# Two modulation sums ordered behind the last turned block, and a Newton step issued on GpSimd, in a hybrid decoder layer

## The chip, the cores and the metric

The kernel runs on one core of one Trainium2 chip. A core has a matrix engine (TensorE, "PE" in the profile, with its weight loads shown as "PEld"), a vector engine (VectorE, "DVE"), a scalar engine (ScalarE, "ACT"), a general engine (GpSimd, "POOL"), and a queue engine (SyncE, "SP") that here only issues transfers between the memory of the chip and the core's own memory (SBUF). Matmul results go to eight PSUM banks of 128 x 512 float32 each.

The metric is the device time of one execution in microseconds (us). Three executions of the kernel before had a median of 737.48 us (737.26 to 738.08). The profiled execution is a fourth one.

## The reference

One post-norm decoder layer on 512 tokens of width 1024 in float32, conditioned on a vector c. What matters here are the modulation, the first LayerNorm, the up-projection behind it and the last LayerNorm:

```
mod = c @ w_ada + b_ada
sh1, sc1, gt1, sh2, sc2, gt2 = split(mod, 6)
u = x * (1 + sc1) + sh1
...                                  # two attention branches, gates, w_o
x = layer_norm(ALPHA * x + (1 + gt1) * attn_out, ln1_g, ln1_b)
u2 = x * (1 + sc2) + sh2
h = causal_depthwise_conv(u2 @ w_up, conv_w, conv_b)
h_gate, h_val = split(h, 2)
ffn_out = (silu(h_gate) * h_val) @ w_down
x = layer_norm(ALPHA * x + (1 + gt2) * ffn_out, ln2_g, ln2_b)

layer_norm(x) = (x - mean) * rsqrt(var + 1e-5) * g + b
```

## The kernel before, in words

**Matmuls.** Every float32 product is made of three passes of a narrower type: each operand is split into a high part (a copy to fp32r on ACT, `hi_of`) and the rest (a subtraction on DVE, `lo_of`, line 94). `mm3` (lines 140 to 142) multiplies high by high, high weight by low activation (`u2l`), and low weight (`wl`) by high activation.

**Weights.** `weights` (line 151) walks a list of items. A load of an item is issued on SP into one of five buffers `raw`, and waits there until the buffer's last reader has run. ACT then makes `wh` (line 203) and DVE makes `wl` (line 94). Among the items are slices of the modulation matrix: their "processing" is not a split but a sum over the row, `mod_sum` (line 226), a VectorE instruction over 128 x 1024 elements with an accumulator that is read out by a second, short one. Sums with a number `n` below 24 are held back and released behind the last `lo_of`; the eight with `n` from 24 on feed the gate `gt2`, which is wanted only in the down-projection, and had no such order.

**Order.** The transfers of SP keep the order of the program. On the other engines a scheduler puts the instructions in order when the kernel is built, by their dependencies and its own costs; `tc.issue_after(x)` adds an edge so that the instructions inside the block stand behind `x` on the engine of `x`. Each engine then runs its list strictly in order.

**Around the first LayerNorm.** The 512 tokens are four blocks of 128. `o_mm` (line 892) multiplies by w_o, `o_norm` (line 906) adds the residual (line 911), takes statistics (line 912) and calls `ln_stats` for mean and reciprocal root, and scales the rows (line 915). `o_turn` (line 918) transposes a block on PE (line 925), applies scale and shift on ACT (line 928, half 0) and DVE (line 929, half 1) and splits it into `u2h` and `u2l`, the moving operands of the up-projection. The first three up-projections (`NSPLIT`) are run in two halves of the tokens: `up_mm` over tokens 0 to 255 for all three, with the turning of block 3 in between, and then over tokens 256 to 511, which need blocks 2 and 3.

**`ln_stats`** (line 862) takes the mean and variance from the statistics (line 864), a square root on ACT (line 866), adds the epsilon (line 867), inverts (line 868), and makes one Newton step of two instructions over 128 x 1 (lines 869 and 870), all but the root on DVE. It is called for the four blocks of the first LayerNorm, for the first two blocks of the last one (`first_rows`), and for its last two (`tail`, line 1196).

**The end.** The last two blocks of rows are finished by `tail(2)` and `tail(3)`: a centering by line 1202, the multiplication with the reciprocal root by line 1206, and a transfer out on SP. The statistics of block 3 wait for the last matmuls of the program, which come in two pieces of 256 columns (lines 1305 and 1306).

Of the kernel before, what the change touches and what calls it, by code (L numbers as in the profile page):

```python
# [12 lines left out]
ALU = mybir.AluOpType  # L13
# [5 lines left out]
D = 1024  # L19
# [8 lines left out]
EPS = 1e-5  # L28
# [23 lines left out]
def layer_kernel(ctx: ExitStack, tc: tile.TileContext, out, xT, x, c8, wa0, wa1, bcol, w1, wct, wv, bf,  # L52
# [3 lines left out]
    V, S, G, PE = nc.vector, nc.scalar, nc.gpsimd, nc.tensor  # L56
# [14 lines left out]
    cnt, state = [0], {"load": 0, "proc": 0}  # L71

    def nm(s):
        cnt[0] += 1
        return f"{s}_{cnt[0]}"

    def bank():
        return pp.tile([P, 512], F32, name=nm("ps"), tag="ps")
# [8 lines left out]
    def fl(ap):  # L87
        return ap.bitcast(F32)

    def hi_of(o, i, scale=1.0):  # L90
        S.activation(o, i, AF.Copy, scale=scale)

    def lo_of(o, i, hi):
        state["read"] = V.tensor_tensor(o, i, fl(hi), ALU.subtract)  # L94
        return state["read"]
# [40 lines left out]
    def z(dt, s, shape=(P, 512)):  # L136
        return zp.tile(list(shape), dt, name=nm(s), tag="z", bufs=NZ)
# [86 lines left out]
    def mod_sum(w, col, wt, c, e, by=None):  # L224
        o = modr[:, w, col, e : e + 1]
        state["read"] = V.scalar_tensor_tensor(wt[:, c], wt[:, c], 1.0, cbc[:, c] if by is None else by, ALU.mult, ALU.mult, accum_out=o)  # L226
        return state["read"]
# [366 lines left out]

    def ada_proc(n):
        def f(r):
            mod_sum((4, 2, 3, 5)[n // 8], n % 8, r, slice(0, D), 0)
        f.late = n < 24
        return f

# [246 lines left out]
    u2h = u2p.tile([P, KT, 512], F32R, name="u2h", tag="u2h")  # L847
    u2l = u2p.tile([P, KT, 512], F32R, name="u2l", tag="u2l")
# [10 lines left out]
    G.memset(epsc, EPS)  # L859


    def ln_stats(st):
        mv = cons.tile([P, 8], F32, name=nm("mv"), tag="mv", bufs=2)
        V.bn_aggr(mv[:, 0:2], st)
        v, s, y, t = mv[:, 2:3], mv[:, 3:4], mv[:, 4:5], mv[:, 5:6]
        S.activation(s, mv[:, 1:2], AF.Sqrt, bias=epsc)
        V.tensor_scalar_add(v, mv[:, 1:2], EPS)
        V.reciprocal(y, s)
        V.scalar_tensor_tensor(t, y, y, v, ALU.mult, ALU.mult)
        V.scalar_tensor_tensor(y, t, -3.0, y, ALU.add, ALU.mult)  # L870
        return mv[:, 0:1], y

    def ln_row(n):
# [32 lines left out]
    def o_norm(i):  # L906
        xn, ps2 = o_st.pop(i)
        st = cons.tile([P, 2, 6], F32, name=nm("st"), tag="st", bufs=2)
        for e in range(2):
            ps = ps2[e]  # L910
            V.scalar_tensor_tensor(xn[e], xn[e], ALPHA, ps, ALU.mult, ALU.add)
            V.bn_stats(st[:, e, :], xn[e])
        mu, rs = ln_stats(st)
        for e in range(2):
            V.tensor_scalar(xn[e], xn[e], mu, rs, ALU.subtract, ALU.mult)
        x1.append(xn)

    def o_turn(i):
        tb = slice(i * P, (i + 1) * P)
        xn = x1[i]  # L920
        pts = [bank(), bank()]
        ufs = [z(F32, "uf2"), z(F32, "uf2")]
        for e in range(2):
            for q in range(4):
                PE.transpose(pts[e][:, q * P : (q + 1) * P], xn[e][:, q * P : (q + 1) * P], ident)
        for q in range(4):
            c = slice(q * P, (q + 1) * P)
            S.activation(ufs[0][:, c], pts[0][:, c], AF.Identity, bias=bm[:, q : q + 1], scale=gm[:, q : q + 1])
            V.tensor_scalar(ufs[1][:, c], pts[1][:, c], gm[:, q + 4 : q + 5], bm[:, q + 4 : q + 5], ALU.mult, ALU.add)
        for e in range(2):  # L930
            uf = ufs[e].rearrange("p (a b) -> p a b", b=P)
            hi_of(u2h[:, 4 * e : 4 * e + 4, tb], uf)
            lo_of(u2l[:, 4 * e : 4 * e + 4, tb], uf, u2h[:, 4 * e : 4 * e + 4, tb])

    def o_x1(i, e):
        if not lnr:
# [58 lines left out]
    for n in range(2 * FT):  # L995
# [7 lines left out]
        if n in (23, 27):  # L1003
            t = t13[(23, 27).index(n)][:, 0:512]
# [48 lines left out]
    for i in range(2, NB):  # L1053
        o_mm(i, range(KT))
        o_norm(i)
        for t in ((0, 1), (2,))[i - 2]:
            o_turn(t)
# [70 lines left out]
    for n in range(2 * FT):  # L1128
# [27 lines left out]
        t = z(F32, "cv")  # L1156
# [6 lines left out]
        if n % 2 == 1:  # L1163
            g, v = hc
# [18 lines left out]
    r = x1  # L1183
# [11 lines left out]

    def tail(i, st, pieces, eng):
        tb = slice(i * P, (i + 1) * P)
        mu, rs = ln_stats(st[:, 0 : len(pieces), :])
        for e, c0, c1 in pieces:
            c = slice(e * 512 + c0, e * 512 + c1)  # L1200
            v = r[i][e][:, c0:c1]
            V.scalar_tensor_tensor(v, v, mu, lnr[0][:, c], ALU.subtract, ALU.mult)
        for e, c0, c1 in pieces:
            c = slice(e * 512 + c0, e * 512 + c1)
            v = r[i][e][:, c0:c1]
            V.scalar_tensor_tensor(v, v, rs, lnr[1][:, c], ALU.mult, ALU.add)
            eng.dma_start(out[tb, c], v)
# [80 lines left out]
    for n, k in enumerate(wi):  # L1288
        w = weights(k)
        for a, p in enumerate(range(2 * n, min(FP - LATE, 2 * n + 2))):  # L1290
            t = ops[p][3]
# [5 lines left out]
    for i in range(2):  # L1297
        pieces = [(1, 0, 512)] if i == 0 else [(1, 0, 256), (1, 256, 512)]
        for n, (e, c0, c1) in enumerate(pieces):
            ps = bank()[:, 0 : c1 - c0] if i else W1[0]  # L1300
            for q in range(LATE):
                t = ops[FP - LATE + q][3]
                product(ps, t[:, top[i]], t[:, bot[i]], wc[q][0][:, c0:c1], wc[q][1][:, c0:c1], i == 1 and q == 0, q == LATE - 1, i == 0)
            v = r[2 + i][e][:, c0:c1]
# [70 lines left out]
```

## Time and profile before

| | |
|---|---|
| median of three executions | 737.48 us |
| profiled execution | 737.86 us |
| its span, first to last instruction | 736.1 us |
| PE busy | 725.6 us (99%) |
| DVE busy | 599.2 us (81%) |
| ACT busy | 390.0 us (53%) |
| POOL busy | 84.7 us (12%) |
| mean clock granted to PE | 0.998 of full speed |

The span is what the trace sees; the profiled execution's own time is 1.76 us longer. A row of the timeline gives the start in us from the span's beginning, the duration, engine, line, operation, the tile written and the tiles read with their shapes, and in brackets how long the engine stood idle before it and what released it. Instructions of one line that follow each other are merged into one row with a count.

### The profile page before, as it was taken

How to read it: one execution, taken by the hardware profiler on the slowest of the kernel's cores; microseconds unless marked ns; L12 is line 12 of the kernel's file. 1: busy time of each engine (PE TensorE's matmuls, PEld its weight loads, DVE VectorE, ACT ScalarE, POOL GpSimd, SP SyncE). 2: the span in 40 equal slices, each digit the busy share in tenths (PEclk: the TensorE clock that was granted, in tenths of full speed). 3: DMA queues.
4: the chain of work that ended last, by engine and by line, in shares of the span. 5: the costliest groups of instructions: out<-in, count | busy, mean ns of one | idle time of the engine just before them, and what ended most of it. 6: DMA issues, size and time to landing. Idle time of an engine off the chain costs nothing.

```text
span 736.1 us, 9841 instructions
## 1 busy us (share of the span) xinstructions
PE 725.6 (99%) x3441; PEld 606.6 (82%) x3441; DVE 599.2 (81%) x1048; ACT 390.0 (53%) x681; POOL 84.7 (12%) x139
## 2 busy tenths in 40 slices
PE   8999999999999999999999999999999999999995
PEld 5888888888888888888889888888888888888885
DVE  6878789778799896883597989977887778679996
ACT  4566476586886755432065554444454544346550
POOL 1026224343010000000000001000011001000010
PEclk9999999999999999999999999999999999999999
DMA  9943634522431232542074678577799767646733
GB/s 341 404 173 118 225 115 150 194 65 103 150 116 61 112 135 94 201 149 86 1 254 132 225 228 253 171 229 226 208 349 247 214 221 217 215 161 225 233 81 87
DMA packets 45346, 131.96 MB, mean 179 GB/s; under 512 B 6152, under 2 KB 6672, under 8 KB 45296
## 3 DMA queue, kind: packets, MB, share of 16 engines
q1 hardware_dynamic: 38032, 112.61, 44.3%
q0 software_dynamic: 4224, 10.30, 7.1%
q10 hardware_dynamic: 3040, 8.42, 3.1%
q8 instruction: 27, 0.44, 0.3%
q14 instruction: 23, 0.19, 0.1%
HBM read 118.39 MB, written 12.85 MB: 178 GB/s over the span
## 4 chain that ended last, share of the span: by engine, by line
PE 94%; DVE 3%; DMA 1%; ACT 1%; issue 0%; DVEq 0%; ACTq 0%
PE ps L140 19%; PE ps L141 19%; PE ps L142 19%; PE ps L342 5%; PE ps L1105 5%; PE ps L1107 5%; PE ps L1106 5%; PE ps L580 3%; PE ps L562 2%; PE ps L488 2%; PE ps L490 2%; PE ps L489 2%; PE ps L903 1%; PE ps L902 1%; PE ps L904 1%; PE ps L514 1%
## 5 line engine op out<-in xcount | busy, mean ns | idle before, releaser
L94 DVE TENSOR_TENSOR wl<-raw,wh 128x1024 fp32r<-128x1024 f32 (+2 forms) x114 | 136.6, 1200 | 34.7 <-ACT wh L203 33.5
L203 ACT ACTIVATE wh<-raw 128x1024 fp32r<-128x1024 f32 (+1 forms) x105 | 109.1, 1041 | 103.7 <-PE ps L141 37.6
L141 PE MATMUL ps<-u2l,wh 128*128 128x512 f32 (+1 forms) x376 | 141.2, 376 | 0.3 <-DVE u2l L94 0.3
L142 PE MATMUL ps<-u2h,wl 128*128 128x512 f32 (+1 forms) x376 | 141.1, 375 | 0.0
L140 PE MATMUL ps<-u2h,wh 128*128 128x512 f32 (+1 forms) x376 | 141.0, 376 | 0.0
L141 PEld LDWEIGHTS ps<-u2l,wh 128*128 128x128 f32 x376 | 70.8, 188 | 13.2 <-DVE u2l L94 0.5
L142 PEld LDWEIGHTS ps<-u2h,wl 128*128 128x128 f32 x376 | 70.8, 188 | 12.9
L140 PEld LDWEIGHTS ps<-u2h,wh 128*128 128x128 f32 x376 | 70.6, 188 | 12.7
L140 PE MATMUL ps<-uh,wh 128*128 128x512 f32 x200 | 79.5, 397 | 0.0
L142 PE MATMUL ps<-uh,wl 128*128 128x512 f32 x200 | 78.2, 391 | 0.0
L141 PE MATMUL ps<-ul,wh 128*128 128x512 f32 x200 | 77.9, 390 | 0.0
L1158 ACT ACTIVATE cv<-ps,cw 128x512 f32<-128x512 f32 x44 | 34.0, 773 | 49.1 <-PE ps L142 39.3
L1159 DVE SCALAR_TENSOR_TENSOR cv<-ps,cw,cv 128x511 f32<-128x511 f32 x44 | 32.8, 745 | 24.8 <-ACT cv L1158 24.7
L142 PEld LDWEIGHTS ps<-uh,wl 128*128 128x128 f32 x200 | 37.5, 188 | 8.5 <-DVE wl L94 0.2
L141 PEld LDWEIGHTS ps<-ul,wh 128*128 128x128 f32 x200 | 37.6, 188 | 7.4
L140 PEld LDWEIGHTS ps<-uh,wh 128*128 128x128 f32 x200 | 37.5, 188 | 7.3
L226 DVE SCALAR_TENSOR_TENSOR raw<-raw,cbc 128x1024 f32<-128x1024 f32 x32 | 39.6, 1238 | 0.0
L542 POOL TENSOR_TENSOR pt<-pt,om 128x127 f32<-128x127 f32 (+3 forms) x32 | 39.0, 1230 | 1.1 <-DVE om L541 1.0
L169 POOL DMA_DIRECT2D raw<-in_wdp x10 | 8.9, 890 | 246.4 <-DMA raw<-in_wdp 228.8
L1160 DVE SCALAR_TENSOR_TENSOR cv<-ps,cw,cv 128x510 f32<-128x510 f32 x44 | 32.7, 744 | 0.4
L1166 ACT ACTIVATE cv<-cv 128x512 f32<-128x512 f32 x22 | 13.9, 631 | 31.7 <-DVE cv L1160 31.7
L541 DVE TENSOR_TENSOR_SCAN om<-om,dg 128x127 f32<-128x127 f32 (+3 forms) x32 | 27.3, 913 | 3.6 <-ACT om L536 3.6
(234 smaller groups left out, 1555.3 us busy)
## 6 DMA issues: line engine op xcount, KB each, us to landing
raw<-in_wup SPq DMA_DIRECT2D x44, 512.0 KB, 4.5
raw<-in_wa SPq DMA_DIRECT2D x32, 512.0 KB, 3.6
raw<-in_wct SPq DMA_DIRECT2D x25, 512.0 KB, 4.4
raw<-in_wdp SPq DMA_DIRECT2D x20, 512.0 KB, 5.3
wa<-in_wa SPq DMA_DIRECT2D x15, 512.0 KB, 7.6
raw<-in_wdp SPq DMA_DIRECT2D x22, 256.0 KB, 4.3
raw<-t SPq DMA_DIRECT2D x22, 256.0 KB, 4.3
raw<-in_wdp POOLq DMA_DIRECT2D x10, 512.0 KB, 7.4
```

What stands on the lines that cost most here:

```text
L94: state["read"] = V.tensor_tensor(o, i, fl(hi), ALU.subtract)
L140: PE.matmul(ps, wh, ah, start=first, stop=False)
L141: PE.matmul(ps, wh, al, start=False, stop=False)
L142: return PE.matmul(ps, wl, ah, start=False, stop=last)
L203: state["hi"] = S.activation(h[:, 0:cols], r[:, 0:cols], AF.Copy)
L226: state["read"] = V.scalar_tensor_tensor(wt[:, c], wt[:, c], 1.0, cbc[:, c] if by is None else by, ALU.mult, ALU.mult, accum_out=o)
L342: PE.matmul(grp[g], w, u, start=j == 0 and n == 0, stop=j == KT - 1 and n == (1 if g == 7 else 2))
L542: G.tensor_tensor(pt[b][:, s : e - 1], pt[b][:, s : e - 1], om[:, s + 1 : e], ALU.mult)
L1105: PE.matmul(ps, ah, bh, start=first, stop=False, skip_group_check=onto)
L1106: PE.matmul(ps, ah, bl, start=False, stop=False, skip_group_check=onto)
L1107: return PE.matmul(ps, al, bh, start=False, stop=last, skip_group_check=onto)
L1158: S.activation(t, ps, AF.Identity, bias=cw[:, n, 3:4], scale=cw[:, n, 2:3])
```

## The change

Three edits. The modulation sums are put behind the last `lo_of` of `o_turn` (numbers from 24 on) or behind the last `lo_of` at all (below 24, which `release` did already). The two instructions of the Newton step become `tensor_scalar` with two per-partition scalars instead of `scalar_tensor_tensor`. And `ln_stats` takes an engine for the epsilon and the Newton step, which is GpSimd in `tail` and VectorE elsewhere.

```diff
     def ada_proc(n):
         def f(r):
-            mod_sum((4, 2, 3, 5)[n // 8], n % 8, r, slice(0, D), 0)
+            with tc.issue_after(state["turn" if n >= 24 else "read"].ins):
+                mod_sum((4, 2, 3, 5)[n // 8], n % 8, r, slice(0, D), 0)
         f.late = n < 24
         return f
...
-    def ln_stats(st):
+    def ln_stats(st, eng=V):
         mv = cons.tile([P, 8], F32, name=nm("mv"), tag="mv", bufs=2)
         V.bn_aggr(mv[:, 0:2], st)
         v, s, y, t = mv[:, 2:3], mv[:, 3:4], mv[:, 4:5], mv[:, 5:6]
         S.activation(s, mv[:, 1:2], AF.Sqrt, bias=epsc)
-        V.tensor_scalar_add(v, mv[:, 1:2], EPS)
+        eng.tensor_scalar_add(v, mv[:, 1:2], EPS)
         V.reciprocal(y, s)
-        V.scalar_tensor_tensor(t, y, y, v, ALU.mult, ALU.mult)
-        V.scalar_tensor_tensor(y, t, -3.0, y, ALU.add, ALU.mult)
+        eng.tensor_scalar(t, y, y, v, ALU.mult, ALU.mult)
+        eng.tensor_scalar(y, t, -3.0, y, ALU.add, ALU.mult)
         return mv[:, 0:1], y
...
-            lo_of(u2l[:, 4 * e : 4 * e + 4, tb], uf, u2h[:, 4 * e : 4 * e + 4, tb])
+            state["turn"] = lo_of(u2l[:, 4 * e : 4 * e + 4, tb], uf, u2h[:, 4 * e : 4 * e + 4, tb])
...
     def tail(i, st, pieces, eng):
         tb = slice(i * P, (i + 1) * P)
-        mu, rs = ln_stats(st[:, 0 : len(pieces), :])
+        mu, rs = ln_stats(st[:, 0 : len(pieces), :], G)
```

With the new edges the scheduler orders DVE and ACT anew around the turning of blocks 2 and 3. The first place is VectorE at the first three up-projection weights. `wl_3778`, `wl_3785` and `wl_3815` are the low parts for up-projections 0, 1 and 2; `xn_3676` is half 1 of block 3. Before:

```order
L94 TENSOR_TENSOR wl_3778<-raw_3767,wh_3777 128x1024
L94 TENSOR_TENSOR wl_3785<-raw_3769,wh_3784 128x1024
L911 SCALAR_TENSOR_TENSOR xn_3676<-xn_3676,ps_3680 128x512
L94 TENSOR_TENSOR wl_3815<-raw_3771,wh_3814 128x1024
L912 BN_STATS st_3729<-xn_3676 128x6
L929 TENSOR_SCALAR uf_722_3746<-ps_3744,gm,bm 128x128
```

On VectorE at the same place, now:

```order
L94 TENSOR_TENSOR wl_3778<-raw_3767,wh_3777 128x1024
L912 SCALAR_TENSOR_TENSOR xn_3676<-xn_3676,ps_3680 128x512
L94 TENSOR_TENSOR wl_3785<-raw_3769,wh_3784 128x1024
L913 BN_STATS st_3729<-xn_3676 128x6
L930 TENSOR_SCALAR uf_722_3746<-ps_3744,gm,bm 128x128
```

The residual of block 3 has moved ahead of `wl_3785`, and `wl_3815` has left this stretch. The second place is VectorE a little later, where block 2 (`uf_721`, `uf_722`) is split, block 3 is scaled (`xn_3675`, `xn_3676`) and turned (`uf_740`, `uf_741`), and the two sums over `raw_3775` and `raw_3979` stand. Before:

```order
L94 TENSOR_TENSOR u2l<-uf_721_3745,u2h 128x4x128
L915 TENSOR_SCALAR xn_3675<-xn_3675,mv_3734 128x512
L915 TENSOR_SCALAR xn_3676<-xn_3676,mv_3734 128x512
L94 TENSOR_TENSOR u2l<-uf_722_3746,u2h 128x4x128
L226 SCALAR_TENSOR_TENSOR raw_3775,modr<-raw_3775,cbc 128x1024
L226 SCALAR_TENSOR_TENSOR raw_3979,modr<-raw_3979,cbc 128x1024
L929 TENSOR_SCALAR uf_741_3845<-ps_3843,gm,bm 128x128 x4
L94 TENSOR_TENSOR u2l<-uf_740_3844,u2h 128x4x128
L94 TENSOR_TENSOR u2l<-uf_741_3845,u2h 128x4x128
L94 TENSOR_TENSOR wl_3982<-raw_3773,wh_3981 128x1024
```

On VectorE there, now:

```order
L94 TENSOR_TENSOR u2l<-uf_721_3745,u2h 128x4x128
L871 TENSOR_SCALAR mv_3734<-mv_3734 128x1
L94 TENSOR_TENSOR u2l<-uf_722_3746,u2h 128x4x128
L916 TENSOR_SCALAR xn_3675<-xn_3675,mv_3734 128x512
L916 TENSOR_SCALAR xn_3676<-xn_3676,mv_3734 128x512
L94 TENSOR_TENSOR wl_3815<-raw_3771,wh_3814 128x1024
L930 TENSOR_SCALAR uf_741_3845<-ps_3843,gm,bm 128x128 x4
L94 TENSOR_TENSOR u2l<-uf_740_3844,u2h 128x4x128
L94 TENSOR_TENSOR u2l<-uf_741_3845,u2h 128x4x128
L226 SCALAR_TENSOR_TENSOR raw_3775,modr<-raw_3775,cbc 128x1024
L226 SCALAR_TENSOR_TENSOR raw_3979,modr<-raw_3979,cbc 128x1024
L94 TENSOR_TENSOR wl_3982<-raw_3773,wh_3981 128x1024
```

The two sums have gone from ahead of the turning of block 3 to behind it, the second split of block 2 has gone ahead of the scaling of block 3, and `wl_3815` now stands between that scaling and the turning. On ScalarE, `wh_3814` went from ahead of the four `uf_721` instructions to behind them. On PE the first matmuls of up-projections 1 and 2 over tokens 256 to 511, which stood ahead of up-projection 0's second matmul there, went back to their own groups. The third place is VectorE at the last rows (block 3, `xn_3675` and `xn_3676`, with statistics `mv_6895`). Before:

```order
L864 BN_AGGR mv_6895<-st_6776 128x2
L867 TENSOR_SCALAR mv_6895<-mv_6895 128x1
L1202 SCALAR_TENSOR_TENSOR xn_3675<-xn_3675,mv_6895,ln_0_5201 128x512
L868 RECIPROCAL mv_6895<-mv_6895 128x1
L1202 SCALAR_TENSOR_TENSOR xn_3676<-xn_3676,mv_6895,ln_0_5201 128x256
L869 SCALAR_TENSOR_TENSOR mv_6895<-mv_6895 128x1
L1202 SCALAR_TENSOR_TENSOR xn_3676<-xn_3676,mv_6895,ln_0_5201 128x256
L870 SCALAR_TENSOR_TENSOR mv_6895<-mv_6895 128x1
L1206 SCALAR_TENSOR_TENSOR xn_3675<-xn_3675,mv_6895,ln_1_5203 128x512
L1206 SCALAR_TENSOR_TENSOR xn_3676<-xn_3676,mv_6895,ln_1_5203 128x256 x2
```

On VectorE there, now:

```order
L865 BN_AGGR mv_6895<-st_6776 128x2
L1203 SCALAR_TENSOR_TENSOR xn_3675<-xn_3675,mv_6895,ln_0_5201 128x512
L869 RECIPROCAL mv_6895<-mv_6895 128x1
L1203 SCALAR_TENSOR_TENSOR xn_3676<-xn_3676,mv_6895,ln_0_5201 128x256 x2
L1207 SCALAR_TENSOR_TENSOR xn_3675<-xn_3675,mv_6895,ln_1_5203 128x512
L1207 SCALAR_TENSOR_TENSOR xn_3676<-xn_3676,mv_6895,ln_1_5203 128x256 x2
```

And the end of GpSimd's list, now, where before nothing stood behind the transfers:

```order
L1266 DMA out<-xn_3459 128x512
L1266 DMA out<-xn_3460 128x512
L868 TENSOR_SCALAR mv_6828<-mv_6828 128x1
L870 TENSOR_SCALAR mv_6828<-mv_6828 128x1
L871 TENSOR_SCALAR mv_6828<-mv_6828 128x1
L868 TENSOR_SCALAR mv_6895<-mv_6895 128x1
L870 TENSOR_SCALAR mv_6895<-mv_6895 128x1
L871 TENSOR_SCALAR mv_6895<-mv_6895 128x1
```

Three instructions of each of the last two blocks (`mv_6828` is block 2) have left VectorE for GpSimd.

## Rows read from the trace of the kernel before

**Rows 1.** Waits of PE, whole run: engine line, releaser: us in total, times, longest

```profile
PE ps L141 <- DVE u2l L94: 0.3, 1, 0.3
```

**Rows 2.** DVE timeline, 381 to 392: start us, us, engine line op out<-in xcount

```profile
381.03 0.68 DVE L911 SCALAR_TENSOR_TENSOR xn<-xn,ps 128x512 f32<-128x512 f32 x1
381.63 1.22 DVE L94 TENSOR_TENSOR wl<-raw,wh 128x1024 fp32r<-128x1024 f32 x1
...
385.74 1.00 DVE L915 TENSOR_SCALAR xn<-xn,mv 128x512 f32<-128x512 f32 x2
386.66 0.69 DVE L94 TENSOR_TENSOR u2l<-uf,u2h 128x512 fp32r<-128x512 f32 x1
387.26 1.22 DVE L226 SCALAR_TENSOR_TENSOR raw<-raw,cbc 128x1024 f32<-128x1024 f32 x1
...
389.55 1.36 DVE L929 TENSOR_SCALAR uf<-ps,gm,bm 128x128 f32<-128x128 f32 x4
390.83 1.47 DVE L94 TENSOR_TENSOR u2l<-uf,u2h 128x512 fp32r<-128x512 f32 x2
```

**Rows 3.** PE timeline, 380 to 392

```profile
380.12 0.39 PE L904 MATMUL ps<-woh,ml 128*128 128x512 f32 x1
...
388.10 0.28 PE L142 MATMUL ps<-u2h,wl 128*128 128x256 f32 x1
...
390.73 0.52 PE L140 MATMUL ps<-u2h,wh 128*128 128x256 f32 x3
391.57 0.39 PE L141 MATMUL ps<-u2l,wh 128*128 128x256 f32 x1 [0.32 <-DVE u2l L94]
```

**Rows 4.** ACT timeline, the high part of the third up-projection weight

```profile
380.07 1.06 ACT L203 ACTIVATE wh<-raw 128x1024 fp32r<-128x1024 f32 x1 [0.21 <-DMA raw<-in_wup]
```

**Rows 5.** SP and DVE timelines: second sum's load, and an addition at 404

```profile
382.87 0.33 SPq L162 DMA_DIRECT2D raw<-in_wa  x1
...
404.44 0.69 DVE L956 TENSOR_TENSOR raw<-raw,raw 128x512 f32<-128x512 f32 x1
```

**Rows 6.** DVE and ACT timelines, last rows, 728 to the end

```profile
728.37 0.42 DVE L1305 TENSOR_TENSOR xn<-xn,ps 128x256 f32<-128x256 f32 x1 [0.29 <-PE ps L1107]
729.29 0.24 DVE L864 BATCH_NORM_AGGREGATE mv<-st 128x2 f32<-128x18 f32 x1
729.56 0.15 DVE L867 TENSOR_SCALAR mv<-mv 128x1 f32<-128x1 f32 x1
729.62 0.29 ACT L866 ACTIVATE mv<-mv,epsc 128x1 f32<-128x1 f32 x1 [4.95 <-DVE mv L864]
729.63 0.74 DVE L1202 SCALAR_TENSOR_TENSOR xn<-xn,mv,ln 128x512 f32<-128x512 f32 x1
730.29 0.16 DVE L868 RECIPROCAL mv<-mv 128x1 f32<-128x1 f32 x1
730.75 0.21 DVE L869 SCALAR_TENSOR_TENSOR mv<-mv 128x1 f32<-128x1 f32 x1
730.88 0.48 DVE L1202 SCALAR_TENSOR_TENSOR xn<-xn,mv,ln 128x256 f32<-128x256 f32 x1
731.27 0.15 DVE L870 SCALAR_TENSOR_TENSOR mv<-mv 128x1 f32<-128x1 f32 x1
731.46 1.54 DVE L1206 SCALAR_TENSOR_TENSOR xn<-xn,mv,ln 128x512 f32<-128x512 f32 x3
```

**Rows 7.** POOL timeline, three multiplications of the attention stage

```profile
56.75 2.66 POOL L542 TENSOR_TENSOR pt<-pt,om 128x127 f32<-128x127 f32 x1
...
60.24 0.63 POOL L542 TENSOR_TENSOR pt<-pt,om 128x255 f32<-128x255 f32 x1
...
60.87 1.08 POOL L542 TENSOR_TENSOR pt<-pt,om 128x511 f32<-128x511 f32 x1
```

**Rows 8.** POOL and DVE timelines, 67 to 71

```profile
67.77 2.06 POOL L542 TENSOR_TENSOR pt<-pt,om 128x511 f32<-128x511 f32 x1
...
68.82 2.10 DVE L94 TENSOR_TENSOR wl<-raw,wh 128x1024 fp32r<-128x1024 f32 x1
```

## Prediction

> **What bounds the kernel now.** I read the waits first, since the page has PE busy for 99% of the span. In the whole run PE waits once for data behind the start-up: 0.3 us, for a low part of block 3 (`u2l`) from DVE [rows 1]. So nothing that makes another engine quicker between the first microseconds and the last matmul can give more than that wait and what follows from it; and anything that makes a weight or an activation late costs in full. The timeline of PE shows the place: three matmuls that need only `u2h`, then a gap of 0.32 us, then a matmul that takes 0.39 where the same shape takes 0.28 [rows 3]. Wait and slow restart are 0.32 + 0.11 = 0.43 us. The timeline of DVE shows what the wait hangs on: two sums from 387.26 to 389.55, 2.29 us, then four scalings and the splits [rows 2]. Of these 2.29 us PE feels 0.43, because it had other matmuls to do.
>
> The second place is the end. Behind the last matmul DVE alone sets the time: subtraction and statistics of the last 256 columns from 728.37, aggregate, root, centering, Newton step, and from 731.46 the last multiplications, each followed by its transfer [rows 6]. There every microsecond of DVE is one of the time.
>
> **Part 1, the sums.** They leave the stretch ahead of block 3, but the order shows that they don't leave alone, so I follow DVE through it. The residual `xn_3676` now stands ahead of `wl_3785`. PE's last matmul for it ends at 380.12 + 0.39 = 380.51 [rows 3], so it starts near 380.5 instead of 381.03, with DVE idle for a moment before. One weight split stands between it and its statistics before and after, so all that follows is 0.5 us early. Then the second split of block 2 goes ahead of the two scalings of block 3: + 0.60 (from 386.66 to 387.26) [rows 2]. The scalings, done at 386.66 before, are done at 386.66 - 0.5 + 0.6 = 386.8, or up to 0.5 later, since ACT now makes the third `wh`, 1.06 us [rows 4], between block 2's scalings and its `u2h` and root, on which DVE waits. Only now comes `wl_3815`, 1.22 us [rows 2]: ready between 388.0 and 388.5. PE wanted it at 388.10 [rows 3]. So a new wait of 0 to 0.5 us comes in; I take 0.3 and the restart of 0.11 with it.
>
> Behind it the four scalings of block 3 take 1.28 (389.55 to 390.83), and with ACT's part the splits come at about 390.3 and 391.0. PE gets to block 3 at 390.73 plus the new wait, and wants the second split 1.5 us after the first (12 matmuls of 0.12, since 22 lie between 388.10 and 390.73). The old wait is gone. Sum of part 1: -0.43 + 0.41, about 0. Bounds: -0.43 if `wl_3815` is in time, and +0.3 if it is as late as 388.5 and its weight load adds some 0.2.
>
> The sums run from about 391. The second needs a load whose buffer is freed by `wl_3815`; it was issued at 382.87 and had landed when its sum began, half of 2.29 us behind 387.26, so 5.5 us later at most, and is now issued near 388.3 and lands by 393.8 [rows 2, 5]. Behind that sum on DVE stands `wl_3982`, which is ready some 2.5 us later, at 396 to 397; PE wants it after 72 more matmuls, near 399.6. On SP the next two transfers wait for the sums and start 4 to 5 us later; what they bring is added on DVE at 404.44 [rows 5]. If that came late, DVE would stand still for at most that long, and PE works on weights that were split before. I cost both at nothing; without this cover the price is the lateness, some 1 us.
>
> **Part 2, the form of the Newton step.** Two `scalar_tensor_tensor` of 0.21 and 0.15 become `tensor_scalar`, of which the nearest row is 0.15 [rows 6]. That is 0 to 0.06 us for each of six calls. They lie under PE's matmuls: nothing.
>
> **Part 3, the last rows on GpSimd.** DVE loses three instructions. What they hold up, from their start to the next one's: 0.07 (729.56 to 729.63), 0.13 (730.75 to 730.88), 0.19 (731.27 to 731.46) [rows 6]: 0.39 us. DVE is free for the last multiplications at 731.07 instead of 731.46. But these now wait for GpSimd, whose two last instructions wait for the reciprocal. The reciprocal ends at 730.29 - 0.07 + 0.16 = 730.38. So the chain DVE to GpSimd, two instructions, and back has 0.69 us for the full gain and 1.08 us before it costs.
>
> The trace of before has no such instruction on GpSimd. Two two-input ones with DVE not in the way take 0.63 at 255 and 1.08 at 511 elements [rows 7]: a line through them gives 0.2 at one element. A hand-over between engines is 0.09 (the aggregate's end, 729.29 + 0.24, to ACT's root, 729.62) [rows 6]. Two instructions and three hand-overs: 0.7 us, so the last multiplications start at 731.07: -0.39.
>
> Against that stands one thing that the trace shows. At 67.77 a GpSimd multiplication of 511 elements takes 2.06 instead of 1.08, and a DVE split under way beside it, with both inputs in SBUF, takes 2.10 instead of 1.22 [rows 2, 7, 8]: they hold each other up, and neither passes the other in the middle. The centerings by line 1202 also have two inputs in SBUF. If each GpSimd instruction must find a gap between them: the epsilon behind the 512-wide centering, done at 730.4; the first centering of 256 columns to 730.8; the next GpSimd instruction 731.0; the second centering 731.4; the last GpSimd instruction 731.6; multiplication at 731.65, +0.2. If DVE's three centerings all go first, three instructions and three hand-overs come after 731.07: 0.9 us, 731.97, +0.5. Between -0.39 and +0.5 I take +0.1, as the row at 68.82 is nearest.
>
> The Trainium skill has this as a rule ("SBUF — State Buffer", section "Who interferes with whom"): a VectorE instruction with two SBUF inputs and a GpSimd instruction that reads SBUF take a shared port in turn, whole instructions at a time. The trace agrees, with 2.10 us against 1.22; by the rule in full the last rows come out at the +0.2 above, without it at -0.39.
>
> Block 2's rows have the same chain. There DVE stands idle for 0.29 before 728.37 [rows 6] and loses 0.39 us of work, so 0.68 us of lateness cost nothing; the chain, with 512-wide centerings, is about that late. I cost it at 0, with +0.3 as the other end.
>
> **Sum.** 0 + 0 + 0.1, about 0.1 us on a profiled execution of 737.86 us. The three executions had a median of 737.48, 0.38 lower, so the forecast for a median is 737.5 us: no change that can be measured. A change below about 0.2%, 1.5 us, can't be told from none here.
>
> **The rivals.**
> - Both gains come in full: `wl_3815` in time and GpSimd within 0.69 us. -0.43 - 0.39 = -0.8: 736.7 us. For it: 0.2 us for a small GpSimd instruction; against it: rows 8, and the place of `wl_3815`. This is the most that the change can give, and still below 1.5 us. Chance 0.2.
> - Slower: GpSimd's chain becomes the bound of the last rows. Place: the last multiplications' wait. It costs from 1.08 us behind the reciprocal on. The first multiplication of GpSimd in the program, 127 elements, took 2.66 us beside DVE scans [rows 7]; one such instruction in the chain puts it at 0.09 x 3 + 0.2 + 2.66 = 3.1 us, +2.1: 739.6 us. Against it: the same line gives 0.2. Chance 0.07.
> - The late transfers stop DVE, and PE after it: +1: 738.5 us. Against it: DVE has a fifth of its time free. Chance 0.05.
> - The change does not do what it says: the pin concerns eight sums, of which two move; the other six stand where they stood. That is in the forecast.
>
> The Trainium skill ("GPSIMD Engine Reference", section "Instruction dispatch") adds about 6 us for the first call of a freshly loaded GpSimd routine; with that the time would be near 743. The trace does not bear it out for the plain instructions, whose first multiplication took 2.66 us.
>
> **How the numbers follow.** Forecast 0.68 (737.5, its own range 736.9 to 738.1), full gain 0.2, GpSimd 0.07, transfers 0.05. The range 736.6 to 738.6 takes in the full gain, both ends of the port's cost and the transfers, and leaves out GpSimd's long chain and small unknowns. Only the GpSimd case and part of the transfers are slower by over 0.2%: 0.08. No case here gives a gain of 1.5 us; for what I don't see I leave 0.04. Within: 0.88.
>
> **What would show it.** Right: PE's wait for `u2l` is gone and one for `wl`, 0.2 to 0.5 us, stands near 388; the sums lie at 391 to 395 and nobody waits for them; the last multiplications start 3.0 to 3.6 us behind the last matmul's subtraction (3.09 before). Wrong: PE shows no wait there and the last multiplications start 2.7 us behind (full gain); or DVE idles over 0.5 us for GpSimd in the last rows; or a new wait of PE stands between 391 and 728. A median below 736 or above 739 would mean that some other stage has changed.

## The result and the profile after

The changed kernel has a median of 738.99 us (738.63 to 740.45, 22 runs), the kernel before, timed beside it, 737.88 us (737.22 to 738.70, 22 runs): 1.11 us more, ratio 1.0016 with a 95% interval of 1.0010 to 1.0022. That is less than the 0.2% that I called measurable, but it lies above the predicted range, and with so many runs it is a loss and no noise. The profiled execution took 739.42 us, its span 737.6 us.

**The middle.** The waits of PE in the whole run, as engine, line and releaser, then us in total, times, longest:

```profile
PE ps L215 <- DVE warm L106: 1.2, 1, 1.2
PE ps L220 <- DVE chl L120: 1.0, 1, 1.0
PE ps L1106 <- DVE cv L1161: 0.3, 1, 0.3
PE ps L342 <- ACT uh L303: 0.3, 1, 0.3
```

The wait for `u2l` [rows 1] is gone. Three of these four lie in the first 15 us; the one at L1106, in the down-projection, is new. The timeline of DVE after, at the stretch of [rows 2] (start us, us, engine, line, operation):

```profile
386.36 1.00 DVE L916 TENSOR_SCALAR xn<-xn,mv 128x512 f32<-128x512 f32 x2
387.27 1.22 DVE L94 TENSOR_TENSOR wl<-raw,wh 128x1024 fp32r<-128x1024 f32 x1
388.41 1.36 DVE L930 TENSOR_SCALAR uf<-ps,gm,bm 128x128 f32<-128x128 f32 x4
390.12 1.29 DVE L94 TENSOR_TENSOR u2l<-uf,u2h 128x512 fp32r<-128x512 f32 x2 [0.35 <-ACT u2h L91]
391.33 1.22 DVE L226 SCALAR_TENSOR_TENSOR raw<-raw,cbc 128x1024 f32<-128x1024 f32 x1
```

The sums stand behind the splits of block 3, and the third `wl` is done at 387.27 + 1.22 = 388.49. PE after, at the stretch of [rows 3]:

```profile
388.26 0.28 PE L141 MATMUL ps<-u2l,wh 128*128 128x256 f32 x1
388.55 0.39 PE L142 MATMUL ps<-u2h,wl 128*128 128x256 f32 x1
388.77 0.28 PE L140 MATMUL ps<-u2h,wh 128*128 128x256 f32 x1
```

From 388.26 to 388.55 are 0.29 us where neighbours are 0.12 apart, and the matmul behind takes 0.39: PE stands for `wl`, as predicted, and loses 0.17 + 0.11 = 0.28 us. The list of waits does not show it; the timeline does. No matmul of block 3 waits for `u2l` any more.

**The end.** The timeline after, around the last matmul (L1108), rows of all engines, to be held against [rows 6]:

```profile
726.79 1.42 DVE L1207 SCALAR_TENSOR_TENSOR xn<-xn,mv,ln 128x512 f32<-128x512 f32 x2 [0.62 <-POOL mv L871]
...
728.12 0.41 DVE L1306 TENSOR_TENSOR xn<-xn,ps 128x256 f32<-128x256 f32 x1
728.44 0.28 PE L1108 MATMUL ps<-wdh,hv 128*128 128x256 f32 x1
728.57 0.43 DVE L1307 BATCH_NORM_STATS2 st<-xn 128x6 f32<-128x256 f32 x1
728.92 0.40 DVE L1306 TENSOR_TENSOR xn<-xn,ps 128x256 f32<-128x256 f32 x1
...
730.09 0.75 DVE L1203 SCALAR_TENSOR_TENSOR xn<-xn,mv,ln 128x512 f32<-128x512 f32 x1
730.14 0.77 POOL L868 TENSOR_SCALAR mv<-mv 128x1 f32<-128x1 f32 x1 [3.39 <-DVE mv L865]
...
730.76 0.15 DVE L869 RECIPROCAL mv<-mv 128x1 f32<-128x1 f32 x1
730.83 0.86 DVE L1203 SCALAR_TENSOR_TENSOR xn<-xn,mv,ln 128x256 f32<-128x256 f32 x2
731.10 0.73 POOL L870 TENSOR_SCALAR mv<-mv 128x1 f32<-128x1 f32 x1 [0.19 <-DVE mv L869]
731.93 0.27 POOL L871 TENSOR_SCALAR mv<-mv 128x1 f32<-128x1 f32 x1
732.23 1.54 DVE L1207 SCALAR_TENSOR_TENSOR xn<-xn,mv,ln 128x512 f32<-128x512 f32 x3 [0.54 <-POOL mv L871]
```

The same place before:

```profile
725.90 0.41 DVE L1305 TENSOR_TENSOR xn<-xn,ps 128x256 f32<-128x256 f32 x1
...
726.35 0.43 DVE L1306 BATCH_NORM_STATS2 st<-xn 128x6 f32<-128x256 f32 x1
...
728.06 0.28 PE L1107 MATMUL ps<-wdh,hv 128*128 128x256 f32 x1
```

From the last matmul's start to the last multiplications it was 731.46 - 728.06 = 3.40 us [rows 6]; it is 732.23 - 728.44 = 3.79. Of these 0.39 us, 0.17 are block 2's: its multiplications waited 0.62 us for GpSimd, so DVE gets to the subtraction at 728.92 without having been idle in front of it, 0.48 behind the matmul instead of 0.31. The order has a part in this too: the subtraction and statistics of the 256 columns ahead of the last ones ran at 725.90 and 726.35 before, ahead of block 2's multiplications; now they stand behind these, at 728.12 and 728.57, so nothing fills the 0.62 us. The other 0.22 are block 3's own chain.

But 0.39 is not 1.11. The rest lies behind the last computing instruction, in the instructions that close the program; no view that I had read goes there. The view of the line on which the program's context is opened and closed (L1371, now L1372) shows them: engine's queue, operation and count, shortest, median and longest duration in ns, first and last start in us. Before:

```profile
L1371 POOLq EVENT_SEMAPHORE  x4: 17/17/17, 735.4 to 736.0; - x4
L1371 POOLq DRAIN  x3: 46/93/7866, 717.0 to 735.8; - x3
L1371 SPq DRAIN  x3: 7/7/7, 735.3 to 735.6; - x3
```

After:

```profile
L1372 POOLq EVENT_SEMAPHORE  x4: 17/17/17, 736.9 to 737.5; - x4
L1372 POOLq DRAIN  x3: 46/98/4991, 731.9 to 737.4; - x3
L1372 SPq DRAIN  x3: 7/7/7, 736.0 to 737.1; - x3
```

Each engine closes its list with a drain, and then all meet at semaphores. SP's first drain comes 0.14 us behind the landing of the last transfer out: 735.3 before, 736.0 after. GpSimd's long drain began at 717.0 before, with its last transfer issue, and ended at 717.0 + 7.87 = 724.9, ten microseconds ahead of SP. After, it begins with the last Newton instruction and lasts from 731.87 to 731.87 + 4.99 = 736.86: 0.83 us behind SP. The semaphores follow at 735.4 before, right behind SP, and at 736.9 after, right behind GpSimd. From the last matmul's start to the span's end it is 8.04 us before and 9.21 us after, 1.17 us more.

### The profile page after: what moved, and what is told of

The parts are those of the page before. It is cut to its first block, busy times and chain, and to the rows that moved or that the text cites. A ratio compares the mean times of both kernels' runs of the same rounds, so it can differ in the third digit from the quotient of the medians.

```text
span 737.6 us, 9846 instructions
## 1 busy us (share of the span) xinstructions
PE 725.9 (98%) x3441; PEld 606.6 (82%) x3441; DVE 599.2 (81%) x1042; ACT 389.5 (53%) x681; POOL 88.5 (12%) x145
## 4 chain that ended last, share of the span: by engine, by line
PE 93%; DVE 3%; DMA 1%; ACT 1%; issue 1%; POOL 0%; DVEq 0%; POOLq 0%; ACTq 0%
PE ps L140 19%; PE ps L142 19%; PE ps L141 19%; PE ps L342 5%; PE ps L1106 4%; PE ps L1107 4%; PE ps L1108 4%; PE ps L580 3%; PE ps L562 2%; PE ps L904 2%; PE ps L905 2%; PE ps L903 2%; PE ps L488 2%; PE ps L490 1%; PE ps L489 1%; PE ps L514 1%
```

## The experiments

The theory that I formed from this: **D**, the drain. GpSimd's closing drain ends about 4.7 us behind its last instruction, and the program 0.8 us behind the later of that drain and SP's. The rivals: **C**, the chain on GpSimd that DVE waits for is the whole cost; **M**, the reordered middle costs it (called U in the expectations on record); **W**, more than one of these. Ratios are to the kernel before on the same chip, with their 95% intervals; 0.0001 is 0.07 us.

**One GpSimd instruction for which nobody waits** (`e5_dummy_newton`), added to the kernel before:

```diff
+    late_s = const([P, 1], F32, "late_s")
...
         mu, rs = ln_stats(st[:, 0 : len(pieces), :])
+        if i == 3:
+            G.tensor_scalar_add(late_s, rs, 0.0)
```

> The kernel before with one more GpSimd instruction (128x1, a copy of the last rows' reciprocal root into a spare column) that nobody waits for; all else stands in the same order. Theory D (end of program: GpSimd's closing drain ends about 4.7 us behind its last instruction, and the program ends only then): the instruction runs beside a two-input multiplication of VectorE and ends near 732.2, the drain near 736.9, so 0.8 us more than before: 738.7 us against 737.9. Theory C (only VectorE's wait for GpSimd's result costs): nobody waits, so no change, 737.9. Theory U (the new order around blocks 2 and 3 costs): no change, 737.9.

739.51 us, ratio 1.0017 (1.0008 to 1.0026): more than the 0.8 us that I wrote for D, and as much as the whole change. Its timeline row and closing rows:

```profile
731.17 0.78 POOL L1202 TENSOR_SCALAR late_s<-mv 128x1 f32<-128x1 f32 x1 [13.35 <-DVE mv L870]
```

```profile
L1375 POOLq DRAIN  x3: 46/98/5497, 731.1 to 737.1; - x3
L1375 SPq DRAIN  x3: 7/7/7, 734.9 to 736.9; - x3
```

The drain ends at 736.6, 1.7 us behind SP. The instruction took 0.78 us beside the last multiplications of DVE, as I had expected; what I had wrong was a sum. I held the drain's end, 736.9, against the old end of the span, 736.1, and left out the 0.8 us that the program takes behind the drain. With them D gives 1.6 us; from the last matmul's start to the span's end this trace has 9.70 instead of 8.04, 1.67 more. DVE waits for nothing new here, so C and M have no part in this kernel.

**The same, behind the last output column** (`e6_dummy_last`):

```diff
+    late_s = const([P, 1], F32, "late_s")
...
+        if i == 3:
+            G.tensor_scalar_add(late_s, v[:, c1 - c0 - 1 : c1 - c0], 0.0)
```

> The kernel before with one more GpSimd instruction (128x1, a copy of the last column that the last multiplication writes) that nobody waits for. Theory D: it starts near 733.1, behind VectorE's last instruction, runs alone and so takes 0.27 us as the lone one in the changed kernel did, and the drain ends near 738.1: 2.0 us more than before, 739.9 us against 737.9. Theories C and U: no change, 737.9. If the shared port makes GpSimd's 0.7 us, the instruction here takes 0.27 and the one beside the multiplication about 0.7; if 0.7 is its own cost, both take 0.7.

740.30 us, ratio 1.0030 (1.0019 to 1.0041):

```profile
732.84 0.23 POOL L1211 TENSOR_SCALAR late_s<-xn 128x1 f32<-128x1 f32 x1 [14.93 <-DVE xn L1208]
```

```profile
L1375 POOLq DRAIN  x3: 46/98/4952, 732.8 to 738.3; - x3
L1375 SPq DRAIN  x3: 7/7/7, 735.0 to 738.0; - x3
```

The 2.0 us that I wrote for D lack the same 0.8; the ratio is 2.2 us (1.4 to 3.0), and this trace has 2.7 more behind the last matmul. The instruction ends 1.13 us later than in the run before, and the span 1.1 us later (738.5 and 737.4): the price follows the place of the last instruction. It took 0.23 us here, with DVE done, and 0.78 there, so the 0.78 are not its own length.

**Another kind of instruction** (`e11_memset_late`): a memset that only writes, over a column that the last Newton instruction has read.

```diff
+        state['t'] = t
...
+        if i == 3:
+            G.memset(state["t"], 0.0)
```

> The kernel before with one GpSimd instruction of another kind behind its end: a memset of 128 x 1 that only writes, over a scratch column that the last Newton instruction has read; nobody waits for it. Drain theory (the closing drain of GpSimd ends 4.67 us behind its last instruction, of whatever kind): the memset ends near 731.6, the drain near 736.3, about 1 us behind SyncE's last wait, so +0.5 to +1.0 us, ratio 1.0007 to 1.0014. Theory that only computing instructions that share the port with VectorE bring the cost: the memset is not held, the drain ends ahead of SyncE's, ratio 1.000.

739.04 us, ratio 1.0014 (1.0005 to 1.0023). It starts 3.42 us behind the last matmul's start, which is 731.5 by the clock of the kernel before, where I had it; this execution is 0.7 us later ahead of that:

```profile
732.20 0.10 POOL L1201 MEMSET mv<- 128x1 f32 x1 [13.33 <-DVE mv L870]
```

```profile
L1374 POOLq DRAIN  x3: 46/93/4779, 732.2 to 737.5; - x3
L1374 SPq DRAIN  x3: 7/7/7, 736.0 to 737.2; - x3
```

A tenth of a microsecond of GpSimd, and the drain still ends at 737.0, 1.0 us behind SP. It is not the kind of instruction that counts.

**Block 3 back on VectorE** (`e3_gps_block2`), block 2 left on GpSimd, the rest as changed:

```diff
-        mu, rs = ln_stats(st[:, 0 : len(pieces), :], G)
+        mu, rs = ln_stats(st[:, 0 : len(pieces), :], G if i == 2 else V)
```

> The changed kernel with the epsilon and the Newton step of the very last rows (block 3) back on VectorE; block 2's stay on GpSimd. Theory D: GpSimd's last instruction ends near 726.7 and the drain near 731.4, long before the last transfer, so of the 1.1 us all but block 2's wait is gone: 738.0 us (737.7 to 738.2). Theory C: the last rows' wait of 0.5 us is gone, block 2's stays, some 0.4 us less than the changed kernel: 738.6. Theory U: 738.6 to 739.0.

738.30 us, ratio 1.0003 (0.9994 to 1.0012): four fifths of the loss are gone with three instructions of 128 x 1.

```profile
L1372 POOLq DRAIN  x3: 46/93/4987, 726.2 to 736.2; - x3
L1372 SPq DRAIN  x3: 7/7/7, 735.7 to 736.0; - x3
```

The drain now ends at 731.2 and holds nobody.

**Only the epsilon on GpSimd** (`e8_eps_gps`), the kernel before otherwise:

```diff
-    def ln_stats(st):
+    def ln_stats(st, eng=V):
...
-        V.tensor_scalar_add(v, mv[:, 1:2], EPS)
+        eng.tensor_scalar_add(v, mv[:, 1:2], EPS)
...
-        mu, rs = ln_stats(st[:, 0 : len(pieces), :])
+        mu, rs = ln_stats(st[:, 0 : len(pieces), :], G)
```

> The kernel before with only the epsilon of the last two blocks on GpSimd (one 128x1 instruction each); Newton step on VectorE in the old form, no pin. Theory D: the instruction runs beside the 512-wide centering and ends near 730.4, the drain near 735.1, just under SP's end at 735.3: no loss from the drain, VectorE 0.07 shorter, but its first Newton instruction waits for nothing new: 737.8 to 738.1. Theory that any GpSimd work in the last rows costs over 1 us: 739.

738.30 us, ratio 1.0002 (0.9993 to 1.0010).

```profile
730.38 0.78 DVE L1202 SCALAR_TENSOR_TENSOR xn<-xn,mv,ln 128x512 f32<-128x512 f32 x1
...
730.42 0.21 POOL L867 TENSOR_SCALAR mv<-mv 128x1 f32<-128x1 f32 x1 [4.45 <-DVE mv L864]
```

Its last GpSimd instruction ends at 730.63 and its drain at 735.30, 0.75 us ahead of SP. I had expected a narrower miss: the instruction took 0.21 us beside a centering of DVE, where the same one for block 2 took 0.78. With 0.78 here too, the drain would still have ended some 0.2 us ahead of SP. So late work on GpSimd is free here when it ends 5.4 us ahead of SP's drain, and by D whenever it ends more than 4.66 us ahead.

From the records of these traces, in us from each span's start ("end" is the span's end, "tail" is counted to it from the last matmul's start, since the runs differ by up to 1.8 us ahead of that; "without the pin" is the kernel without the order of the sums, and "old form in front" the one with the old form on VectorE, both below):

| kernel | last GpSimd instruction ends | GpSimd's drain ends | SP's first drain | end | tail |
|---|---|---|---|---|---|
| before | 718.15 (a transfer issue) | 724.87 | 735.27 | 736.09 | 8.04 |
| epsilon only | 730.63 | 735.30 | 736.04 | 736.87 | 8.00 |
| block 2 only | 726.52 | 731.18 | 735.66 | 736.49 | 8.29 |
| after | 732.19 | 736.86 | 736.03 | 737.65 | 9.21 |
| without the pin | 731.83 | 736.49 | 735.67 | 737.28 | 9.20 |
| old form in front | 730.85 | 735.51 | 734.69 | 736.30 | 9.22 |
| extra instruction | 731.95 | 736.61 | 734.91 | 737.41 | 9.70 |
| extra, last column | 733.07 | 737.74 | 735.00 | 738.53 | 10.73 |
| memset | 732.30 | 736.96 | 735.98 | 737.75 | 8.98 |

In all eight kernels with a late instruction the drain ends 4.66 to 4.67 us behind it, and each span ends 0.79 to 0.83 us behind the later of the two drains. D is shown, and it is the larger part of the loss: SP is done 7.59 us behind the last matmul's start instead of 7.22, which is C's 0.37, and the drain adds 0.83 less 0.03 of a shorter closing, 0.80. Together they are the 1.17 us.

**The parts without each other.** `e2_gps_only` is the change without the order of the sums:

```diff
-            with tc.issue_after(state["turn" if n >= 24 else "read"].ins):
-                mod_sum((4, 2, 3, 5)[n // 8], n % 8, r, slice(0, D), 0)
+            mod_sum((4, 2, 3, 5)[n // 8], n % 8, r, slice(0, D), 0)
```

> The changed kernel without the pin on the sums (GpSimd and the new form stay; one of the two sums goes back ahead of block 3's turning). Theories C and D: the cost is in the last rows, 739.0 us as the changed kernel, or up to 0.4 more for the sum that PE's block 3 waits for again. If the pin were the cause: back to 737.9.

739.09 us, ratio 1.0014 (1.0005 to 1.0023), nearly that of the whole. `e4_form_only` has nothing but the new form; `eng` is VectorE at every call:

```diff
-        V.scalar_tensor_tensor(t, y, y, v, ALU.mult, ALU.mult)
-        V.scalar_tensor_tensor(y, t, -3.0, y, ALU.add, ALU.mult)
+        eng.tensor_scalar(t, y, y, v, ALU.mult, ALU.mult)
+        eng.tensor_scalar(y, t, -3.0, y, ALU.add, ALU.mult)
```

> The kernel before with the new form of the Newton step alone (all on VectorE, no pin). The build order shows that this form, not the pin, moves the residual of block 3, the third weight's low part and one of the sums. Theory: new wait of 0.3 us near 388 and, since one sum still stands ahead of block 3, perhaps part of the old one: 738.0 us (737.8 to 738.3). Theory U: 738.6 to 739.0.

738.47 us, ratio 1.0002 (0.9993 to 1.0011). `e1_pin_only` has the order of the sums and the new form, all on VectorE:

```diff
-        mu, rs = ln_stats(st[:, 0 : len(pieces), :], G)
+        mu, rs = ln_stats(st[:, 0 : len(pieces), :])
```

> The changed kernel with the last rows' epsilon and Newton step back on VectorE: pin and new form stay. Theory D and C: all of the 1.1 us is gone, and what is left is the middle: the old wait of 0.43 us gone, a new one of about 0.3 for the third weight's low part: 737.7 us (737.5 to 737.9). Theory U: 738.6 to 739.0.

738.42 us, ratio 1.0003 (0.9994 to 1.0012): the gain of 0.2 us that I expected of it doesn't show, though the interval would hold it. `e7_pin_old_form` has the order of the sums alone, with the old form:

```diff
-            mod_sum((4, 2, 3, 5)[n // 8], n % 8, r, slice(0, D), 0)
+            with tc.issue_after(state["turn" if n >= 24 else "read"].ins):
+                mod_sum((4, 2, 3, 5)[n // 8], n % 8, r, slice(0, D), 0)
...
-            lo_of(u2l[:, 4 * e : 4 * e + 4, tb], uf, u2h[:, 4 * e : 4 * e + 4, tb])
+            state["turn"] = lo_of(u2l[:, 4 * e : 4 * e + 4, tb], uf, u2h[:, 4 * e : 4 * e + 4, tb])
```

> The kernel before with the pin alone: the Newton step keeps its old form and VectorE. In the build order only the two sums move (behind block 3's splits), and two early matmuls of PE go back to their groups. If PE's wait for block 3 is what the sums cost: the wait of 0.32 us and the slow restart go, 0.4 us less than before, 737.5 us against 737.9. If the pin were harmful (later loads): 738.0 to 738.9.

737.71 us, ratio 0.9994 (0.9985 to 1.0002). `e9_pin_again` is the same kernel, timed a second time:

> The pin alone once more, with the Newton step in its old form on VectorE: the same kernel as in the run before, on another chip visit, to narrow its interval. It left GpSimd's list alone, so the drain theory and the theory of GpSimd's chain both expect no cost at the end. Taken from the first run (0.9994): 0.3 to 0.6 us below the kernel before, ratio 0.9992 to 0.9996, from the 0.43 us of wait and restart at PE's u2l. If the first run was noise: 1.0000.

737.85 us, ratio 0.9993 (0.9985 to 1.0002). Both runs lie 0.0006 to 0.0007 below 1, some 0.5 us, though each interval by itself still holds 1. Two of the waits of PE, both of the start-up, and DVE in the middle:

```profile
PE ps L220 <- POOL epsc L860: 1.3, 1, 1.3
PE ps L215 <- DVE warm L106: 1.2, 1, 1.2
```

```profile
388.47 1.36 DVE L930 TENSOR_SCALAR uf<-ps,gm,bm 128x128 f32<-128x128 f32 x4 [1.19 <-PE ps L926]
390.24 1.29 DVE L94 TENSOR_TENSOR u2l<-uf,u2h 128x512 fp32r<-128x512 f32 x2 [0.41 <-ACT u2h L91]
391.45 1.22 DVE L226 SCALAR_TENSOR_TENSOR raw<-raw,cbc 128x1024 f32<-128x1024 f32 x1
```

No `wl` stands ahead of the four scalings; DVE even has 1.19 us to spare there, and no wait of PE is listed behind the start-up. The orders in which these kernels are built say why: with the order of the sums alone the third `wl` stays where it was before. It is the new form of the two instructions, without any pin, that makes the scheduler put `wl_3815`, `xn_3676` and the second split of block 2 elsewhere. The trace of `e4_form_only`, which has no pin, shows the third `wl` at the late place:

```profile
387.40 1.22 DVE L94 TENSOR_TENSOR wl<-raw,wh 128x1024 fp32r<-128x1024 f32 x1
```

The traces also give the size of all this. From the first transposition of block 3 on PE to the first matmul of the down-projection it is 39.61 us in each of the four kernels with the pin and the old form in front (`e7_pin_old_form`, `e9_pin_again`, `e10_pin_eps_act`, `e12_old_front`) and 39.87 to 39.91 in the five with the new form, with the pin or without it. The five with neither take 39.73 (`e5_dummy_newton`), 39.78 (`e6_dummy_last`), 40.18 (the kernel before), 40.24 (`e11_memset_late`) and 40.76 (`e8_eps_gps`), with the same order on PE, DVE and ACT up to there. So the wait for `u2l` is another one in each execution, and the 0.32 us of [rows 3] are one draw of it; in the two slowest the second sum itself waits for its load, 0.44 and 0.83 us. The pin saves 0.12 to 1.15 us of this, 0.5 on the mean.

**The changed kernel with the old form on VectorE** (`e12_old_front`). Ahead of the last rows every engine's order is that of `e9_pin_again`, so against that kernel it is the GpSimd part alone:

```diff
-        eng.tensor_scalar(t, y, y, v, ALU.mult, ALU.mult)
-        eng.tensor_scalar(y, t, -3.0, y, ALU.add, ALU.mult)
+        if eng is G:
+            eng.tensor_scalar(t, y, y, v, ALU.mult, ALU.mult)
+            eng.tensor_scalar(y, t, -3.0, y, ALU.add, ALU.mult)
+        else:
+            V.scalar_tensor_tensor(t, y, y, v, ALU.mult, ALU.mult)
+            V.scalar_tensor_tensor(y, t, -3.0, y, ALU.add, ALU.mult)
```

> The changed kernel with the Newton step's old form wherever VectorE makes it; GpSimd has the last rows as in the changed kernel. Ahead of the last rows every engine's order is then that of the pin alone. Theory that the cost is all at the end (0.39 us of chain and 0.75 us of drain) and that the order brought by the new form costs something too: 1.1 us above the pin alone (0.9993), so ratio 1.0006 to 1.0010, about 0.5 us below the changed kernel; no wait of PE behind the start-up for u2l or cv. Theory that the form's order costs nothing: ratio 1.0014 to 1.0018, as the changed kernel. In both, GpSimd's drain ends 4.67 us behind its last instruction and the program 0.8 us behind that, 9.2 us behind the last matmul's start.

738.78 us, ratio 1.0007 (0.9998 to 1.0016). The end is as both theories had it, and no wait of PE for `u2l` or `cv` is listed. The ratio is the first theory's, but the interval holds the other's 1.0014 too.

```profile
730.58 0.27 POOL L872 TENSOR_SCALAR mv<-mv 128x1 f32<-128x1 f32 x1
```

```profile
L1376 POOLq DRAIN  x3: 46/93/4989, 730.5 to 736.0; - x3
```

Three pairs that differ by the GpSimd part alone (this kernel and `e9_pin_again`, the changed one and `e1_pin_only`, `e2_gps_only` and `e4_form_only`) agree on its price: 1.0007 - 0.9993, 1.0016 - 1.0003 and 1.0014 - 1.0002 are 0.0014, 0.0013 and 0.0012, or 0.9 to 1.0 us, each with some 0.0012 on either side, where the traces give 1.1 to 1.2.

**A version that beats both** (`e10_pin_eps_act`): the order of the sums with the old form, and the epsilon of the last two blocks on ScalarE. Against the changed kernel, in part:

```diff
-        eng.tensor_scalar_add(v, mv[:, 1:2], EPS)
+        if late:
+            S.activation(v, mv[:, 1:2], AF.Identity, bias=epsc)
+        else:
+            V.tensor_scalar_add(v, mv[:, 1:2], EPS)
...
-        mu, rs = ln_stats(st[:, 0 : len(pieces), :], G)
+        mu, rs = ln_stats(st[:, 0 : len(pieces), :], True)
```

> The pin alone, and in the last two blocks the epsilon is added by ScalarE instead of VectorE; GpSimd does nothing at the end. If VectorE's list alone sets the last rows, the 0.07 us that the epsilon holds up the first centering is gained and nothing else: ratio to the kernel before 0.0001 below that of the pin alone, last multiplications 3.0 us behind the last subtraction instead of 3.09. If the hand-over from ScalarE is late, the same as the pin alone. No theory expects a drain that ends behind SyncE's.

737.58 us, ratio 0.9988 (0.9980 to 0.9997), the only kernel here whose interval lies below 1. Its last rows:

```profile
728.76 0.42 DVE L1309 TENSOR_TENSOR xn<-xn,ps 128x256 f32<-128x256 f32 x1 [0.34 <-PE ps L1111]
...
730.21 0.28 ACT L869 ACTIVATE mv<-mv,epsc 128x1 f32<-128x1 f32 x1
...
731.78 1.54 DVE L1210 SCALAR_TENSOR_TENSOR xn<-xn,mv,ln 128x512 f32<-128x512 f32 x3
```

The last multiplications start 3.02 us behind the subtraction instead of 3.09 [rows 6]: the 0.07 us of the epsilon. Of the 0.0012, the order of the sums has 0.0006 to 0.0007; the rest is within what the intervals leave open, and so is the question whether this kernel is faster than the one with the pin alone.

## Why the prediction was wrong

**The step that failed is part 3**, "Between -0.39 and +0.5 I take +0.1", and with it the sentence that it rests on: "Behind the last matmul DVE alone sets the time". The bounds were of a chain of computing instructions and ended at the last multiplications. I had the row on GpSimd's list, "where before nothing stood behind the transfers", and took it for an idle engine. It had a closing drain behind it, which the trace of before shows with 7.87 us and 10 us of slack to SP's. The change moved its start from 717.0 to 731.9 and used up that slack and 0.83 us more. The upper end of +0.5 had to be +1.17, which the three pairs measure as 0.9 to 1.0.

**The chain was mis-sized too.** Block 3's rows came out at +0.22, where I had worked out +0.2 for instructions that must each find a gap between the centerings, and then took +0.1. The size of that bound was right, its path was not: DVE's two centerings of 256 columns ran back to back (0.86 us for both), and the Newton step came behind them. Block 2's rows, "I cost it at 0", cost 0.17, with the order that left DVE idle there. The port behaved as I read it from [rows 8]: instructions of 128 x 1 took 0.77 and 0.73 us beside the centerings, each ending just behind one (730.14 + 0.77 = 730.91 against 730.09 + 0.75 = 730.84), and 0.27 alone. But DVE's centering beside it took 0.75, as before 0.74 [rows 6]: in the changed kernel only GpSimd was held up. In `e8_eps_gps` it went the other way once, with 0.21 for GpSimd and 0.78 for the centering. The Trainium skill ("SBUF — State Buffer", section "Who interferes with whom") adds that a GpSimd instruction that only writes is not held by such a VectorE instruction; the memset, 0.10 us beside the multiplications of DVE, agrees, since memsets of this size take 0.09 to 0.10 us elsewhere in the kernel before.

**Part 1 had the place right, both sizes somewhat off and the cause wrong.** -0.43 + 0.41 = 0 was forecast. The wait for `wl` is at 388.5 as predicted and the old one is gone, but the new one costs 0.28 and not 0.41. The old one was mis-read: the matmul that waits starts 0.60 us behind the one ahead of it where neighbours are 0.12 apart, so PE lost 0.48 + 0.11 = 0.59 and not 0.43. The profiled executions have 39.88 in the middle against 40.18, a gain of 0.3, inside my bounds; the kernel with the new order and the new form, all on VectorE, measures 1.0003 (0.9994 to 1.0012). And I laid the reorder to the new edges, here and in the section on the change. The edges alone leave `wl_3815` where it was, and measure 0.9994 and 0.9993. I had compared the whole change with the kernel before, not its parts.

**Part 2, "nothing", missed two prices of the new form.** One is the order: 0.26 to 0.30 us in the middle over the old form with the pin. The other is the instructions themselves, which I had 0 to 0.06 us shorter, from a row that adds a constant. On VectorE they are longer: 0.27 and 0.20 us in the changed kernel's first LayerNorm (at 384.86 and 385.64), where the old form takes 0.21 and 0.15 [rows 6]. In `e1_pin_only` and `e4_form_only`, which make them on VectorE in the last rows too, the tail is 8.13 and 8.14 us against 8.03 and 8.04 with the old form; the changed kernel has no such part at its end.

By the ratios the form costs nothing without the pin (1.0002), and with it 0.0009 to 0.0010 in two pairs (1.0003 against 0.9994 and 0.9993; 1.0016 against 1.0007). That is 0.7 us, of which the traces show 0.3 to 0.4. Neither pair alone shows it, as the ratios have 0.0006 to 0.0009 on either side, and the rest is in no stage that I can point at: from the first matmul of the down-projection to the last one it is 300.91 to 301.61 us in the five kernels with the new form and 300.89 to 301.65 in the nine with the old one in front. The late transfers cost nothing that I can find: no wait stands between 391 and 400.

**The rivals.** The slower one put the cost at the right engine and place, but by a slow instruction of 2.66 us in the chain; no instruction took over 0.78. The full gain was excluded by the port, as weighed. "A median below 736 or above 739 would mean that some other stage has changed": 738.99 is at that line, and it was the stage behind the last computing instruction. Of the signs, those of "Right" came about, the wait for `wl` at 388.5, with 0.17 us, and the last multiplications 3.31 us behind the subtraction among them, and one of "Wrong" with them: DVE idles 0.62 and 0.54 us for GpSimd in the last rows. None of them looked behind the last multiplications, where most of the loss was.

**What stays open:** the wait of 0.3 us for `cv` in the down-projection, new in the changed kernel's list. It is listed, with 0.3 to 0.6, in three kernels with the new form (the changed one, `e1_pin_only`, `e4_form_only`), and not in the two others, `e2_gps_only` and `e3_gps_block2`. But the same matmul, near 667, is late with the old form too, by a pause too short for the list: it starts 0.36 to 0.52 us behind the one ahead of it in `e7_pin_old_form`, `e10_pin_eps_act`, `e6_dummy_last` and `e11_memset_late`, where neighbours are 0.23 apart. In `e9_pin_again`, the same kernel as `e7_pin_old_form`, it is 0.27. So the wait is not the new form's alone and changes from one execution to the next; why it was longest with the new form stays open.

## What to carry to other kernels

Follow the chain past the last computing instruction: read when each engine's closing drain ends and which of them the end waits for, before you give late work to an engine that is long done. Work that is free on an engine in the middle can bring in, at the end, its own length and a closing of several microseconds, here 4.66 us. And build each part of a change alone and compare the orders, since a scheduler may answer to an edit that looks harmless, such as another form of the same instruction.

## What the hardware showed that I had not expected

GpSimd's closing drain ends 4.66 to 4.67 us behind its last instruction, whether that is a `tensor_scalar` of 0.21 to 0.78 us or a memset of 0.10 us; behind transfer issues it ended 6.1 to 7.1 us later, in six kernels. The longest closing drains of DVE and ACT end 0.05 and 0.04 us behind their engine's last instruction, in all fourteen traces. And a `tensor_scalar` on one element per partition took GpSimd 0.21 to 0.27 us with no VectorE instruction with two inputs in SBUF in its way, and 0.68 to 0.78 us beside one, but for the 0.21 us in `e8_eps_gps`.
